# Moving elementwise sums to VectorE and reordering the start of the up projection

## The chip, the cores and the metric

The kernel runs on one core of one Trainium2 chip. The metric is the device time of one execution in microseconds (us), as the median of several runs; lower is better. Five engines work in a core, each through its own queue in order: TensorE (PE) multiplies matrices and writes PSUM, VectorE (DVE) and ScalarE (ACT) work element by element, GpSimd (POOL) does so too but reads no PSUM here, and SyncE (SP) issues the DMA transfers.

## The reference

One layer of a diffusion backbone with D = 1024, 1024 latent tokens and 256 context tokens. What comes ahead of the change (adaLN, input projection, mLSTM, windowed attention) is left as it is. What matters here is the end of the layer:

```python
x = x + g_a * (jnp.concatenate([y_m, y_a], axis=-1) @ w_out[l])
x = x + g_f * conv_glu(modulate(rmsnorm(x, norm_ffn[l]), sh_f, sc_f),
                       w_up[l], ffn_conv_w[l], ffn_conv_b[l], w_down[l])
...
def conv_glu(h, w_up, conv_w, conv_b, w_down):
    a, val = jnp.split(h @ w_up, 2, axis=-1)
    a = jax.nn.gelu(dwconv(a, conv_w, conv_b))
    return (a * val) @ w_down
```

`w_up` is 1024 x 5632, `w_down` 2816 x 1024, and the result is normed once more (`final_norm`).

## The kernel before, in words

**Products.** Every f32 operand is split into a high part (an fp32r copy, made on ACT) and a low part (the operand less its high part, made by a subtraction on VectorE or GpSimd). A product is three matmuls: high by high, high by low, low by high.

**The up projection** is done by a two by two scheme with seven products in place of eight. The features (1024) are cut into two halves and the tokens (1024) into two halves; the columns of `w_up` are taken in 22 blocks, each of 128 value columns and 128 gate columns. On the token side the seven operands lie in `hB` (high and low), in slots named B11, B21, B22, T1, T2, T3, T4. B11 and B21 belong to the first four token blocks, B22 to the last four; the T's are sums: `sum1` gives T1 = B12 - B11, `sum2` T2 = B22 - T1, `sum3` T3 = B22 - B12, `sum4` T4 = B21 - T2. `sum1` and `sum4` overwrite the raw tile of block b - 4, `sum3` that of block b. On the weight side a block arrives as `R`, two tiles (`Ra` with two parts, `Rb` with two parts and room for three more). `sums_v` makes two sums in `Rb`, `sums_g` two more; the second of `sums_g` overwrites the part `R[1][:, 1]`, which the first of `sums_v` reads. `wsplit` makes the high and low parts (`wh`, `wl`) of a pair of them: number 0 from `Ra`, 1 from the sums of `sums_v`, 2 and 3 from the rest.

**The loop over token blocks** (from L1450 on; order 1, 5, 2, 6, 3, 7, 4, with block 0 made ahead) does for block b half of the output projection (`wout_n`, 12 matmuls for each half n) and adds it to the residual x (L1361, VectorE); for the block before it the norm (`sq`, `norm_b`: squares and root on ACT, reciprocal on VectorE) and eight transposes (L1391); for the block before that the evacuation (`evac`, L1403 on ACT and L1405 on VectorE, into the raw tile) and the splits into `hB`. With a block of the second half (5, 6, 7) come its token sums. In the loop 5 and 6 have their turn; `split34`, the high and low parts of T3 and T4, runs an iteration later (`late`). Blocks 7 and 4 come behind the loop. The raw tiles of blocks 5 to 7 share one buffer, so the evacuation of block 7 waits until the low part of T3 of block 6 has been read.

**Behind the loop** come the first product of all (`ps_a`, B11), the last norm (block 4, one half on ACT, the other on VectorE, L1377), the transposes of block 4, `ps_a2`, the sums of the first weight block, and the first products f, c, b, e, d of block 0 (B22, T1, T2, T3, T4 in this order).

**Blocks 1 to 21.** Block i runs the products a, b, A, c, e, d, C on PE; A adds into a's PSUM and C into c's. VectorE makes `u2` from b, then in `av2` adds e (to `u3`) and c (to `av`). C writes into c's bank and so has to wait for `av2`. VectorE also does the sums and splits for block i + 1 and the conv, gate and products of block i - 1, with GpSimd taking `mul2` and the sums of `combine`.

**What sets the order.** From the token loop to the end PE, VectorE, ACT and GpSimd run in the order in which the code issues their instructions (a manual schedule called `fence`); SP does so from the first products on. A wait at the head of a queue holds all that is behind it.

Of the kernel before, what the change touches and what calls it, by code (L numbers as in the profile page):

```python
# [18 lines left out]
P = 128  # L19
# [59 lines left out]
def build(tc, I, out, dbg=None):  # L79
    nc = tc.nc  # L80
    dbg = dbg or {}
    V, S, G, T = nc.vector, nc.scalar, nc.gpsimd, nc.tensor
# [889 lines left out]
    for h in range(H):  # L972
# [3 lines left out]
        else:  # L976
            wq = [wkq]
            late = lambda: wq.append(load_split(I["w_q"][1], 256, lambda: pq.tile([P, 4, 256], F32, name="wr", tag="rga")))
# [75 lines left out]
    class Wout:  # L1054
# [21 lines left out]
        def lo(self):  # L1076
            r = lambda a: a[:].rearrange("p (j q) -> p j q", j=4)
            V.tensor_tensor(out=r(self.l), in0=self.src, in1=r(self.h).bitcast(F32), op=ALU.subtract)
# [161 lines left out]
    for t in range(n + 2):  # L1240
        blk, sub = divmod(t, 4)
# [75 lines left out]
    hB = [hbp.tile([P, 7, 4, 512], F32R, name=f"hB{i}") for i in range(2)]  # L1317
    tbk = ExitStack()
    tbp = tbk.enter_context(tc.tile_pool(name="tbp", bufs=1, side="right", reuse_waits="tile"))
    B11, B21, B22, T1, T2, T3, T4 = range(7)  # L1320
# [19 lines left out]
    sub = lambda e, o, x, y: e.tensor_tensor(out=o, in0=x, in1=y, op=ALU.subtract)  # L1340
# [3 lines left out]
    def ysplit_h(b, eng=G):  # L1344
        ys[b] = [t4.tile([P, 4, P], F32R, name=f"y{n}", tag=f"y{n}", bufs=3 if n == "h" else 2) for n in "hl"]
        eng.copy(ys[b][0][:], yslice(b)) if eng is S else eng.tensor_copy(ys[b][0][:], yslice(b))
# [8 lines left out]
    def wout_n(b, n):  # L1355
        ns = slice(512 * n, 512 * n + 512)
        po = pO.tile([P, 512], F32, name="po", tag="o")
        yh, yl = ys[b]
        for kt in range(4):
            mm3(po[:], yh[:, kt], yl[:, kt], wos[4 + kt][0][:, ns], wos[4 + kt][1][:, ns], kt == 0, kt == 3)  # L1360
        return lambda: V.tensor_tensor(out=xs[b][:, ns], in0=po[:], in1=xs[b][:, ns], op=ALU.add)  # L1361
# [31 lines left out]
    def evac(b, kts=None):  # L1393
        w = KT // len(pts[b])
        if b not in raws:
            raws[b] = (tbp.tile([P, 2, 4, P], F32, name="raw00") if b == 0 else
                       er[:].rearrange("p a (k t) -> p a k t", k=4) if b == 4 else
                       tbp.tile([P, 2, 4, P], F32, name="raw", tag=f"raw{b // 4}", bufs=RB1 if b > 4 else 2))
        for kt in kts or range(KT):
            ga, sh = ada2[:, 16 + kt:17 + kt], ada2[:, 8 + kt:9 + kt]  # L1400
            o, i_ = raws[b][:, kt // 4, kt % 4], pts[b][kt // w][:, kt % w]
            if kt // w % 2 == 0:
                S.activation(o, i_, AF.Identity, bias=sh, scale=ga)  # L1403
            else:
                V.tensor_scalar(out=o, in0=i_, scalar1=ga, scalar2=sh, op0=ALU.mult, op1=ALU.add)  # L1405
# [9 lines left out]
    def sum1(b):  # L1415
        sub(V, raws[b - 4][:, 0], raws[b][:, 0], raws[b - 4][:, 0])
# [5 lines left out]
    def sum3(b, e=V):  # L1422
        sub(e, raws[b][:, 0], raws[b][:, 1], raws[b][:, 0])

    def sum4(b, e=V):
        sub(e, raws[b - 4][:, 1], raws[b - 4][:, 1], tbs[b][:, 0])

    def sum34(b):
        sum3(b, G)
        sum4(b, G)  # L1430

    split_t1 = lambda b: split(V, b, T1, 1, raws[b - 4][:, 0:1])
    split_t2 = lambda b: split(V, b, T2, 1, tbs[b][:])
# [9 lines left out]
                sub(V, hB[1][:, blk:blk + 1, :, ts], src, hB[0][:, blk:blk + 1, :, ts].bitcast(F32))  # L1443
        return lo

    def prod(ps, wt, j, blk, first, last, kts=range(4)):
        for kt in kts:
            ks = slice(kt * P, kt * P + P)
            for (sw, part) in ((0, 0), (0, 1), (1, 0)):
                T.matmul(ps[:], wt[sw][:, j, ks], hB[part][:, blk, kt, :], start=first and kt == 0 and sw + part == 0,  # L1450
                         stop=last and kt == 3 and sw == 1, skip_group_check=not first)

    load_x(1)
    order = [1, 5, 2, 6, 3, 7, 4]
# [10 lines left out]
    late = None  # L1465
    last = order[-1]
    for i, b in enumerate(order):
        prev = order[i - 1] if i else None
        pp = order[i - 2] if i > 1 else 0 if i == 1 else None
        add0 = wout_n(b, 0)  # L1470
        if prev is not None:
            sq(prev, 1)
        if pp is not None:
            evac(pp)
        if prev is not None:
            norm_b(prev)
        if i + 2 < len(order):
            ysplit_h(order[i + 2])
        if i + 1 < len(order):
            ysplit_l(order[i + 1])  # L1480
        lo = split(V if b == last else G, pp, B11, 2, raws[pp][:], True) if pp is not None and pp < 4 else None
        add0()
        sq(b, 0)
        if lo:
            lo()
        if late and b != last:
            late()()
            late = None
        if pp is not None and pp >= 4:
            sum1(pp)  # L1490
            sum2(pp)
            sum34(pp)
            split(V, pp, B22, 1, raws[pp][:, 1:2])
            split_t1(pp)
            late = lambda a=pp: split34(a)
        add1 = wout_n(b, 1)
        trans(prev if i else 0)
        add1()
        if pp is not None and pp >= 4:
            split_t2(pp)  # L1500
        if b != last:
            nc.sync.dma_start(x2_d[b][:], xs[b])
        if i + 2 < len(order):
            load_x(order[i + 2])
    ps_a = pA.tile([P, 512], F32, name="pa", tag="a")
    prod(ps_a, e0, 0, B11, True, True)
    lo = late()
    sq(4, 1)
    norm_b(4, True)
    lo()  # L1510
    nc.scalar.dma_start(x2_d[4][:], xs[4])
    evac(7)
    trans(4, (4, 5, 6, 7))
# [12 lines left out]
    f = ExitStack()  # L1526
# [12 lines left out]
    def sums_v(R, e=V):  # L1539
        add(e, R[1][:, 2], R[1][:, 1], R[1][:, 0])  # L1540
        sub(e, R[1][:, 3], R[1][:, 2], R[0][:, 0])


    def sums_g(R, e=V):
        sub(e, R[1][:, 4], R[0][:, 1], R[1][:, 3])
        sub(e, R[1][:, 1], R[0][:, 0], R[1][:, 1])

    def wsplit(R, n, eng=V):
        src = (R[0][:], R[1][:, 2:4], R[1][:, 0:2], R[1][:, 4:5])[n]
        w = src.shape[1]  # L1550
        wt = [fw.tile([P, w, 512], F32R, name=f"w{n}{w}", tag=f"w{n}{w}", bufs=5 if w == 2 else 2) for n in "hl"]
        S.copy(wt[0][:], src)  # L1552
        sub(eng, wt[1][:], src, wt[0][:].bitcast(F32))
        return wt


    R = load_R(0)
    sums_v(R, G)
    sums_g(R, G)
    evac(4, range(4, 8))  # L1560
    sum1(7)
    split(V, 7, B22, 1, raws[7][:, 1:2])
    split(V, 4, B22, 1, raws[4][:, 1:2])
    wB = wsplit(R, 3)
    evac(4, range(4))
    sum1(4)
    wS = wsplit(R, 1)
# [9 lines left out]
    newp = lambda n: (pA if n == "a" else pB if n in "fb" else pC).tile([P, 512], F32, name="p" + n,  # L1577
                                                                    tag={"a": "a", "f": "b", "b": "b"}.get(n, "c"))
    ps0 = {n: newp(n) for n in "fcbed"}
    prod(ps0["f"], wB, 0, B22, True, True)  # L1580
    prod(ps0["c"], wS, 0, T1, True, True)
    prod(ps0["b"], wS, 1, T2, True, True)
    wA = wsplit(R, 2)
# [13 lines left out]
    R = load_R(blocks[1])  # L1597
# [105 lines left out]
    R = load_R(blocks[2])  # L1703


    for i in range(1, NF):
        last = i == NF - 1
        if i > 1:
            C = Block(i, W, B)
            C.pe("a")  # L1710
            C.sn_()
        W = {}

        def split_w(*ns):
            for n in ns:
                if not last:
                    W[n] = wsplit(R, n)

        if i == 1:
            C.pe("b")  # L1720
            C.u2_()
            split_w(0)
            Rn = load_R(blocks[3], (0,))
            B.vt_()
            B.taps()
            B.gelu()
            for n in "Aced":
                C.pe(n)
            C.av2()
            sums_v(R)  # L1730
            C.av1()
            split_w(1)
            B.mul1()
            B.mul2()
            C.ident_()
            sums_g(R)
            B.combine()
            split_w(2, 3)
            R = load_R(blocks[3], (1,), Rn)
            C.pe("C")  # L1740
            B = C
            continue
        B.vt_()
        B.taps()
        B.gelu()
        B.mul1()
        B.mul2()
        C.pe("b")
        C.u2_()
        if not last:  # L1750
            sums_v(R)
        split_w(0)
        C.pe("A")
        C.pe("c")
        if i == NF - 2:
            nc.sync.dma_start(er[:], I["w_down"][0:2 * P, 0:512].rearrange("(k p) f -> p k f", p=P))
            nc.sync.dma_start(ar0[:], act_d["a11", 0][:])
        B.combine()
        if last:
            split2(e0[0][:], e0[1][:], er[:])  # L1760
            split2(a0[0][:], a0[1][:], ar0[:])
        C.pe("e")
        C.pe("d")
        C.av2()
        if last:
            C.pe("C")
            break
        sums_g(R)
        split_w(1)
        Rn = load_R(blocks[i + 2], (0,)) if i < NF - 2 else None  # L1770
        split_w(2)
        C.av1()
        C.ident_()
        split_w(3)
        R = Rn and load_R(blocks[i + 2], (1,), Rn)
        C.pe("C")
        B = C
# [186 lines left out]
    for t, (p, ps, fresh) in enumerate(products):  # L1964
        for j in range(NP):
# [35 lines left out]
            if NP + 3 <= n < NP + 3 + NL:  # L2001
                b = n - NP - 3
# [9 lines left out]
        if p == "m4":  # L2012

            part = lambda f_, *bs: [lambda b=b: f_(b) for b in bs]
# [106 lines left out]
```

## Time and profile before

| | us |
|---|---|
| median of 3 runs | 1279.54 |
| lowest and highest run | 1278.59 and 1282.48 |
| profiled execution, from first to last instruction | 1281.0 |
| PE busy in it | 1240.8 (97%) |
| VectorE busy in it | 974.5 (76%) |
| GpSimd busy in it | 208.8 (16%) |

The profiled execution has no other time than its span. Its times run from its first instruction: the token loop lies at about 582 to 629 us, the first products of block 0 end near 658, block 2 lies at 677 to 701 and block 3 behind it. A row of the timeline has the start, the duration, the engine, the line, the operation, output and inputs by name, shapes, the count of merged instructions, and in brackets how long the engine had stood idle and what ended that. A group's duration of two merged instructions is that of both. The granted clock is a share of TensorE's full speed.

### The profile page before, as it was taken

What the parts mean: (1) busy time and instruction counts of PE and PEld (TensorE: products, weight loads), DVE (VectorE), ACT (ScalarE), POOL (GpSimd) and SP (SyncE); (2) the same over time, 40 slices, a digit from 0 to 9 for tenths busy, and PEclk for the clock granted to TensorE, in tenths of its full rate; (3) what the DMA queues carried; (4) which work ended last, traced back from release to release, by engine and by line L of the source; (5) the groups of instructions that cost most, each with busy time, mean ns of one, the idle gap of its engine ahead of it and who ended that gap; (6) DMA issues with size and microseconds to landing.
All of it is one profiled execution on the core that took longest, in us unless ns stands there. A gap on an engine that the chain in (4) does not pass through costs nothing.

```text
span 1281.0 us, 19212 instructions
## 1 busy us (share of the span) xinstructions
PE 1240.8 (97%) x7023; PEld 1060.6 (83%) x7023; DVE 974.5 (76%) x1679; ACT 638.1 (50%) x1308; POOL 208.8 (16%) x175
## 2 busy tenths in 40 slices
PE   6999999999999999999899999999999999999997
PEld 4799898999898888887677888888888888788886
DVE  5863687877887878776898777777777776867887
ACT  6632556464865777776644333333333334444435
POOL 1200000000001433232402311332321332001000
PEclk9999999999999999999999999999999999999999
DMA  9431544452254332103413222233222337975563
GB/s 361 180 122 35 141 137 143 123 168 77 84 183 162 134 116 67 67 34 132 135 63 110 105 99 95 104 119 108 101 100 99 106 108 261 345 264 172 194 199 135
DMA packets 90416, 175.63 MB, mean 137 GB/s; under 512 B 12938, under 2 KB 29522, under 8 KB 90322
## 3 DMA queue, kind: packets, MB, share of 16 engines
q1 hardware_dynamic: 90034, 173.63, 40.2%
q8 instruction: 55, 0.90, 0.3%
q10 hardware_dynamic: 288, 0.79, 0.2%
q14 instruction: 39, 0.32, 0.1%
HBM read 136.05 MB, written 38.33 MB: 136 GB/s over the span
## 4 chain that ended last, share of the span: by engine, by line
PE 78%; DVE 8%; ACT 5%; DMA 5%; issue 3%; POOL 1%; SPq 0%; DVEq 0%; ACTq 0%; POOLq 0%
PE pd L1958 14%; PE pa L1450 9%; PE pc L1450 9%; PE pp L588 6%; PE pe L1450 4%; PE pb L1450 4%; PE pd L1450 4%; PE u L1174 3%; PE pt L1151 2%; PE po L307 2%; PE pv L307 2%; PE pv L309 2%; PE pv L308 2%; PE po L309 2%; PE po L308 2%
## 5 line engine op out<-in xcount | busy, mean ns | idle before, releaser
L1552 ACT CAST wh<-Rb 128x1024 fp32r<-128x1024 f32 (+1 forms) x66 | 59.5, 903 | 147.7 <-PE pd L1450 83.0
L1958 PE MATMUL pd<-dh,al 128*128 128x512 f32 x296 | 115.4, 390 | 0.7 <-DVE al L1324 0.6
L1958 PE MATMUL pd<-dl,ah 128*128 128x512 f32 x296 | 115.2, 389 | 0.0
L1958 PE MATMUL pd<-dh,ah 128*128 128x512 f32 x296 | 115.2, 389 | 0.0
L1450 PE MATMUL pc<-hB,wh 128*128 128x512 f32 x344 | 107.1, 393 | 2.5 <-DVE av L1529 2.5
L1450 PE MATMUL pa<-hB,wh 128*128 128x512 f32 x336 | 103.6, 390 | 0.0
L1340 DVE TENSOR_TENSOR wl<-Rb,wh 128x1024 fp32r<-128x1024 f32 (+1 forms) x66 | 68.9, 1045 | 39.4 <-ACT wh L1552 38.8
L1660 POOL TENSOR_TENSOR tt<-vt,tt 128x512 f32<-128x512 f32 x22 | 29.5, 1341 | 325.6 <-ACT tt L1654 325.6
L588 PE MATMUL pp<-hl,wh 128*128 128x512 f32 x256 | 79.3, 405 | 0.0
L1450 PEld LDWEIGHTS pc<-hB,wh 128*128 128x128 f32 x344 | 65.3, 190 | 16.6 <-DVE av L1529 2.9
L307 PE MATMUL pv<-wh,hl 128*128 128x256 f32 x256 | 76.1, 297 | 0.5 <-ACT ym L601 0.5
L1450 PEld LDWEIGHTS pa<-hB,wh 128*128 128x128 f32 x336 | 63.2, 188 | 13.6 <-ACT sn L1624 0.4
L309 PE MATMUL pv<-wh,hl 128*128 128x256 f32 x256 | 72.3, 283 | 0.0
L308 PE MATMUL pv<-wl,hl 128*128 128x256 f32 x256 | 72.3, 282 | 0.0
L1450 PE MATMUL pc<-hB,wl 128*128 128x512 f32 x172 | 67.6, 393 | 0.0
L1958 PEld LDWEIGHTS pd<-dh,al 128*128 128x128 f32 x296 | 55.5, 188 | 12.8 <-DVE al L1324 1.4
L1958 PEld LDWEIGHTS pd<-dl,ah 128*128 128x128 f32 x296 | 55.6, 188 | 11.9 <-DVE dl L1324 0.3
L1450 PE MATMUL pa<-hB,wl 128*128 128x512 f32 x168 | 65.4, 389 | 0.0
L1958 PEld LDWEIGHTS pd<-dh,ah 128*128 128x128 f32 x296 | 55.6, 188 | 11.5
L1158 ACT CAST ph<-pt 128x512 fp32r<-128x512 f32 (+1 forms) x88 | 46.2, 525 | 27.0 <-PE pt L1151 26.8
L1139 POOL TENSOR_SCALAR p__4966<-p__4966,ss 128x512 f32<-128x512 f32 x1 | 0.7, 688 | 346.6 <-DVE ss L1136 346.6
L1450 PE MATMUL pe<-hB,wh 128*128 128x512 f32 x176 | 54.6, 390 | 0.4 <-DVE hB L1340 0.2
(1072 smaller groups left out, 3760.2 us busy)
## 6 DMA issues: line engine op xcount, KB each, us to landing
w<-in_w_ada_dram SPq DMA_DIRECT2D x64, 256.0 KB, 2.7
br<-in_w_down_dram SPq DMA_DIRECT2D x25, 512.0 KB, 6.6
Ra<-in_w_up_dram SPq DMA_DIRECT2D x22, 512.0 KB, 3.6
Rb<-in_w_up_dram SPq DMA_DIRECT2D x22, 512.0 KB, 3.5
ar<-act_s SPq DMA_DIRECT2D x44, 256.0 KB, 3.6
act_a<-tt SPq DMA_DIRECT2D x33, 256.0 KB, 2.0
act_s<-tt SPq DMA_DIRECT2D x33, 256.0 KB, 2.0
wr<-in_w_h_dram SPq DMA_DIRECT2D x16, 512.0 KB, 4.4
```

What stands on the lines that cost most here:

```text
L307: T.matmul(ps, st_hi, mv_hi, start=first, stop=False)
L308: T.matmul(ps, st_hi, mv_lo, start=False, stop=False)
L309: T.matmul(ps, st_lo, mv_hi, start=False, stop=last)
L588: T.matmul(pp[:, 512 * n:512 * n + 512], wkq[sw][:, kt, cs], hl[n][part][:, kt, :], start=kt == 0 and sw + part == 0, stop=kt == KT - 1 an ...
L1151: T.transpose(self.pt[i][:, (2 * kk + j) * P:(2 * kk + j + 1) * P], self.p[j][:, kb * P:(kb + 1) * P], ident[:])
L1158: S.copy(self.ph[i][:, :w], self.pt[i][:, :w])
L1174: T.matmul(self.u[:], vv[:, c, self.g], part[i][:, kk * 2 * P:(kk + 1) * 2 * P], start=kb + m == 0, stop=kb == last and m == 1)
L1340: sub = lambda e, o, x, y: e.tensor_tensor(out=o, in0=x, in1=y, op=ALU.subtract)
L1450: T.matmul(ps[:], wt[sw][:, j, ks], hB[part][:, blk, kt, :], start=first and kt == 0 and sw + part == 0, stop=last and kt == 3 and sw == 1 ...
L1552: S.copy(wt[0][:], src)
L1660: G.tensor_tensor(out=self.tt[:, h2_], in0=self.vt[:], in1=self.tt[:, h2_], op=ALU.mult)
L1958: T.matmul(ps[:], ac[sa][:, js], w[sw], start=first and n == 0, stop=last and n == 2, skip_group_check=not fresh)
```

## The change

It has five parts.

1. The third and fourth token sums of blocks 5 and 6 (`sum34`) go from GpSimd to VectorE, and from ahead of the B22 split to behind the low part of T2, which is behind the second add to x.
2. The late parts of T3 and T4 of block 6 are written as a whole, high and low, ahead of the last norm; the low ones stood behind the norm's half on VectorE.
3. Of the four sums of the first weight block three go from GpSimd to VectorE, behind the evacuation of block 7; GpSimd keeps the one that overwrites `R[1][:, 1]`. `sum1` of block 7 goes behind the weight part of the first product.
4. The first product of block 0 (f, B22) runs its twelve matmuls by parts: four high by high, then four with the low tokens, then four with the low weights; before, each of the four 128-feature slices ran its three in a row.
5. In block 2 alone, `sums_v` and the first weight split for block 3 go behind `av2`.

The core of the diff:

```diff
     def sum34(b):
-        sum3(b, G)
-        sum4(b, G)
+        sum3(b)
+        sum4(b)
...
-    def prod(ps, wt, j, blk, first, last, kts=range(4)):
-        for kt in kts:
-            ks = slice(kt * P, kt * P + P)
-            for (sw, part) in ((0, 0), (0, 1), (1, 0)):
-                T.matmul(ps[:], wt[sw][:, j, ks], hB[part][:, blk, kt, :], start=first and kt == 0 and sw + part == 0,
-                         stop=last and kt == 3 and sw == 1, skip_group_check=not first)
+    def prod(ps, wt, j, blk, first, last, by_part=False):
+        parts = ((0, 0), (0, 1), (1, 0))
+        for kt, (sw, part) in ([(kt, p_) for p_ in parts for kt in range(4)] if by_part else
+                               [(kt, p_) for kt in range(4) for p_ in parts]):
+            T.matmul(ps[:], wt[sw][:, j, kt * P:kt * P + P], hB[part][:, blk, kt, :],
+                     start=first and kt == 0 and sw + part == 0, stop=last and kt == 3 and sw == 1,
+                     skip_group_check=not first)
...
             sum1(pp)
             sum2(pp)
-            sum34(pp)
             split(V, pp, B22, 1, raws[pp][:, 1:2])
             split_t1(pp)
             late = lambda a=pp: split34(a)
...
         add1()
         if pp is not None and pp >= 4:
             split_t2(pp)
+            sum34(pp)
...
     prod(ps_a, e0, 0, B11, True, True)
-    lo = late()
+    late()()
     sq(4, 1)
     norm_b(4, True)
-    lo()
...
     R = load_R(0)
-    sums_v(R, G)
-    sums_g(R, G)
+    sums_v(R)
     evac(4, range(4, 8))
-    sum1(7)
+    sub(V, R[1][:, 4], R[0][:, 1], R[1][:, 3])
+    sub(G, R[1][:, 1], R[0][:, 0], R[1][:, 1])
     split(V, 7, B22, 1, raws[7][:, 1:2])
     split(V, 4, B22, 1, raws[4][:, 1:2])
     wB = wsplit(R, 3)
+    sum1(7)
...
-    prod(ps0["f"], wB, 0, B22, True, True)
+    prod(ps0["f"], wB, 0, B22, True, True, True)
...
         B.mul2()
         C.pe("b")
         C.u2_()
-        if not last:
-            sums_v(R)
-        split_w(0)
+        if i > 2:
+            if not last:
+                sums_v(R)
+            split_w(0)
...
         C.av2()
+        if i == 2:
+            sums_v(R)
+            split_w(0)
```

VectorE's order in the loop, in the iteration that sums block 5; the first row is the second add to x, the second T2's low part, and the last two the next norm's scale and the next evacuation:

```order
 L1361 TENSOR_TENSOR x_7611<-po,x_7611 128x512
 L1340 TENSOR_TENSOR hB_7461<-tb,hB_7460 128x4x128
+L1340 TENSOR_TENSOR raw<-raw 128x512
+L1340 TENSOR_TENSOR raw<-raw,tb 128x512
 L1370 TENSOR_SCALAR r_7710<-r_7710 128x1
 L1405 TENSOR_SCALAR raw<-pt,ada_65 128x128 x4
```

The two sums are new in VectorE's queue; the add to x keeps its place ahead of them.

VectorE's order from the last add to x to block 4's evacuation (`er` is block 4's raw tile; the two `hB` rows are the late low parts; L1377 is the norm's half; the `Rb` rows are weight sums):

```order
 L1361 TENSOR_TENSOR x_7816<-po,x_7816 128x512
+L1340 TENSOR_TENSOR hB_7461<-raw,hB_7460 128x4x128 x2
 L1370 TENSOR_SCALAR r_7916<-r_7916 128x1
 L1374 RECIPROCAL r_7916<-r_7916 128x1
 L1377 TENSOR_SCALAR hn<-x_7816,r_7916 128x512
-L1340 TENSOR_TENSOR hB_7461<-raw,hB_7460 128x4x128 x2
 L1405 TENSOR_SCALAR raw<-pt,ada_65 128x128 x4
+L1529 TENSOR_TENSOR Rb<-Rb 128x512
+L1340 TENSOR_TENSOR Rb<-Rb,Ra 128x512
 L1405 TENSOR_SCALAR er<-pt,ada_65 128x128 x2
-L1340 TENSOR_TENSOR raw<-raw 128x512
+L1340 TENSOR_TENSOR Rb<-Ra,Rb 128x512
```

The low parts went ahead of the norm, and three weight sums came in behind block 7's evacuation.

VectorE's order in block 2 (`u_8365` is `u2`, `u_8366` is `u3`; the `Rb` rows are the sums for block 3 and `wl` its first low part):

```order
 L1529 TENSOR_TENSOR u_8365<-pb,sn 128x512
-L1529 TENSOR_TENSOR Rb<-Rb 128x512
-L1340 TENSOR_TENSOR Rb<-Rb,Ra 128x512
-L1340 TENSOR_TENSOR wl_8372<-Ra,wh_8371 128x1024
 L1529 TENSOR_TENSOR u_8366<-pe,u_8365 128x512
 L1529 TENSOR_TENSOR av<-pc,u_8366 128x512
+L1529 TENSOR_TENSOR Rb<-Rb 128x512
+L1340 TENSOR_TENSOR Rb<-Rb,Ra 128x512
+L1340 TENSOR_TENSOR wl_8433<-Ra,wh_8432 128x1024
 L1340 TENSOR_TENSOR Rb<-Ra,Rb 128x512 x2
```

The two adds that C waits for now come first, and the three steps for block 3 behind them.

## The prediction

> **What bounds the kernel now.** I read the page first, then who TensorE (PE) waited for between 600 and 720 us, where all the edits lie, then the granted clock there.
>
> ```profile
> span 1281.0 us, 19212 instructions
> ...
> PE 1240.8 (97%) x7023; PEld 1060.6 (83%) x7023; DVE 974.5 (76%) x1679; ACT 638.1 (50%) x1308; POOL 208.8 (16%) x175
> ```
>
> PE is busy 97% of the span, so only time in which PE stands still, or runs slowly, can be won. The waits of PE (in total, times, longest):
>
> ```profile
> PE pc L1450 <- DVE av L1529: 2.5, 1, 2.5
> PE pt L1391 <- ACT hn L1379: 1.5, 3, 0.5
> PE pt L1391 <- DVE raw L1405: 1.3, 1, 1.3
> PE pf L1450 <- ACT wh L1552: 1.1, 1, 1.1
> PE po L307 <- DVE x L1361: 0.6, 1, 0.6
> PE pt L1391 <- DVE hn L1377: 0.6, 1, 0.6
> ```
>
> These six add to 7.6 us. Two of them cost more than their length. Busy time by stretch (length, PE, PEld, DVE, ACT, POOL, granted clock, DMA share, GB/s):
>
> ```profile
> 642.82:646.24 3.42, 3.42 (x10) 2.65 (x9) 3.35 (x5) 1.41 (x3) 0.00 (x0) 0.50 0.00 0
> 694.03:697.44 3.41, 1.08 (x5) 0.91 (x6) 3.38 (x6) 0.00 (x0) 0.00 (x0) 1.00 0.21 77
> 697.44:700.86 3.42, 3.42 (x10) 2.65 (x9) 3.02 (x4) 1.34 (x2) 0.00 (x0) 0.50 0.48 153
> 702.00:760.00 58.00, 58.00 (x257) 48.01 (x256) 43.51 (x48) 19.56 (x22) 12.52 (x8) 1.00 0.27 96
> ```
>
> After the 2.5 us wait (694 to 696) the clock is 0.50 for 3.42 us, and so it is after the waits of 1.3 and 1.1 us (643 to 646). From 702 on PE never stops. In the chain that ended last the slow stretch is a product of 12 matmuls that took 4.59 us where the same product of the next block took 2.72:
>
> ```profile
> 696.36 4.59 PE pc L1450 x12
> ...
> 717.33 2.72 PE pc L1450 x12
> ```
>
> ```profile
> 693.48 0.39 PE L1450 MATMUL pd<-hB,wl 128*128 128x512 f32 x1
> 696.36 0.73 PE L1450 MATMUL pc<-hB,wh 128*128 128x512 f32 x2 [2.49 <-DVE av L1529]
> ```
>
> So the stall in block 2 is worth 2.49 + (4.59 - 2.72) = 4.36 us. The half clock at 643 is different: there the product behind it waits for VectorE anyway.
>
> ```profile
> 652.68 0.50 PE L1450 MATMUL pe<-hB,wh 128*128 128x512 f32 x1 [0.23 <-DVE hB L1340]
> ```
>
> PE, slow clock included, was at pe before VectorE had written the low part of T3. Between the loop over token blocks and 652 us the end is set by VectorE's queue; each us that leaves this queue moves everything behind it.
>
> **Block 2.** VectorE, PE and GpSimd (POOL) there:
>
> ```profile
> 688.38 0.68 DVE L1529 TENSOR_TENSOR u<-pb,sn 128x512 f32<-128x512 f32 x1
> 689.32 1.72 DVE L1529 TENSOR_TENSOR Rb<-Rb 128x512 f32<-128x512 f32 x1 [0.26 <-DMA Rb<-in_w_up_dram]
> 691.07 1.67 DVE L1340 TENSOR_TENSOR Rb<-Rb,Ra 128x512 f32<-128x512 f32 x1
> 692.66 2.32 DVE L1340 TENSOR_TENSOR wl<-Ra,wh 128x1024 fp32r<-128x1024 f32 x1
> 694.90 0.68 DVE L1529 TENSOR_TENSOR u<-pe,u 128x512 f32<-128x512 f32 x1
> 695.61 0.69 DVE L1529 TENSOR_TENSOR av<-pc,u 128x512 f32<-128x512 f32 x1
> ```
>
> ```profile
> 690.99 0.62 PE L1450 MATMUL pd<-hB,wh 128*128 128x512 f32 x2
> ```
>
> ```profile
> 690.56 3.33 POOL L1340 TENSOR_TENSOR tt<-tt 128x512 f32<-128x512 f32 x2
> ```
>
> The two adds at 694.90 and 695.61 read products e and c; the seventh product writes into c and so waits for the second add. They stand behind two weight sums and a low part (5.6 us) that the next block wants. With the change they go first: e is complete as d starts (691.0, and its last matmul drains until some 691.2), two adds of 0.7 end at 692.6, and PE's d ends at 693.7: no wait. The 4.36 us go. What is late next: the sums start at 692.6 in place of 689.3. One is still beside POOL (1.72), one free (0.64), the low part free (1.21, below); they end near 696.1. The next steps started at 696.2 before, so VectorE is 0 to 0.6 us earlier, while PE is 4.36 earlier. Block 3 had slack for that:
>
> ```profile
> 708.56 1.03 DVE L1529 TENSOR_TENSOR Rb<-Rb 128x512 f32<-128x512 f32 x1
> ...
> 711.21 1.21 DVE L1340 TENSOR_TENSOR wl<-Ra,wh 128x1024 fp32r<-128x1024 f32 x1
> 714.64 0.69 DVE L1529 TENSOR_TENSOR u<-pe,u 128x512 f32<-128x512 f32 x1 [2.22 <-PE pe L1450]
> ```
>
> VectorE stood ready from 712.4 and waited 2.22 us for PE; then the adds took 1.4 us. With PE 4.36 earlier, the seventh product of block 3 comes at 717.33 - 4.36 = 713.0, and VectorE, ready at 711.8 to 712.4, ends the adds at 713.2 to 713.8: a new wait of 0.2 to 0.8 us; I take 0.6. Net gain 3.8 us; at most 4.36, and 2.7 if block 3's low part falls beside POOL (2.32 for 1.21, 1.1 more).
>
> The row behind the clock term is the 0.50 after 2.49 us of idle PE. The Trainium skill, TensorE: Matmul & The Clock Gate, section "Why this matters for your kernels", asks for PE gaps over some 3 us before the clock falls; by that rule the stall would be worth its 2.49 us alone, and the sum 1.9 us less. This trace differs from it twice, and the measurement decides.
>
> **The loop over token blocks.** The third and fourth token sums went to POOL in two iterations, and VectorE's low parts ran beside them:
>
> ```profile
> 605.99 1.79 POOL L1340 TENSOR_TENSOR raw<-raw 128x512 f32<-128x512 f32 x1 [4.39 <-DVE raw L1340]
> ```
>
> ```profile
> 606.61 3.42 DVE L1340 TENSOR_TENSOR hB<-raw,hB 128x512 fp32r<-128x512 f32 x2
> ...
> 622.72 2.72 DVE L1340 TENSOR_TENSOR hB<-raw,hB 128x512 fp32r<-128x512 f32 x2 [0.67 <-ACT hB L1410]
> ...
> 652.54 1.28 DVE L1340 TENSOR_TENSOR raw<-raw,tb 128x512 f32<-128x512 f32 x2
> ```
>
> A pair of 128x512 ops takes 1.28 us alone and 3.42 or 2.72 beside POOL. The change saves 3.42 - 1.28 + 2.72 - 1.28 = 3.6 us of VectorE and adds four sums, 2.6 us: net 1.0. Its y casts stay on POOL and may now fall beside the pairs; I take 0.7, bounds 0 and 1.0. PE's wait for x (0.6) goes, since the add comes ahead of the sums; the sums stand ahead of the next norm, so its waits for hn shrink less.
>
> **Low parts ahead of the last norm.** On VectorE, ScalarE (ACT) and POOL:
>
> ```profile
> 630.89 0.68 DVE L1361 TENSOR_TENSOR x<-po,x 128x512 f32<-128x512 f32 x1
> ...
> 632.89 1.55 DVE L1377 TENSOR_SCALAR hn<-x,r 128x512 f32<-128x512 f32 x1
> 634.35 3.47 DVE L1340 TENSOR_TENSOR hB<-raw,hB 128x512 fp32r<-128x512 f32 x2
> 637.75 1.36 DVE L1405 TENSOR_SCALAR raw<-pt,ada 128x128 f32<-128x128 f32 x4
> ```
>
> ```profile
> 632.36 0.29 ACT L1371 ACTIVATE r<-r 128x1 f32<-128x1 f32 x1
> ```
>
> ```profile
> 632.86 1.28 POOL L1529 TENSOR_TENSOR Rb<-Rb 128x512 f32<-128x512 f32 x1 [7.97 <-DMA Rb<-in_w_up_dram]
> ...
> 635.65 3.30 POOL L1340 TENSOR_TENSOR Rb<-Ra,Rb 128x512 f32<-128x512 f32 x2
> ```
>
> From the last add of x to the evacuation of block 7 are 637.75 - 630.89 = 6.9 us, with norm and low parts beside POOL's weight sums. Changed: add 0.6, low parts 1.3, the square root and its hand-overs 0.7, the norm's half 0.7 (as a free 128x512 op; 1.55 is its locked price) = 3.3. It saves 3.6, bounds 2.7 (norm still locked) and 3.9. The low parts delay the norm by 1.3; what they release, the buffer of block 7's evacuation, is then free ahead of it.
>
> **Weight sums.** Three of four come onto VectorE behind that evacuation; the one left on POOL rewrites a part that the first reads, so it can start only then, beside the second. Price 0.64 + 1.72 + 0.64 = 3.0; bounds 1.9 (no lock) and 4.1 (two). The data had landed at 632.86 and is now asked for near 634, so the load hides; behind its store on SP it even starts earlier. The row here is 1.72 for 0.64. The Trainium skill, SBUF — State Buffer, section "Who interferes with whom", has the second of two such operations wait for the whole of the first; POOL's 1.65 in front of 0.64 would make 2.3, and the sum 0.6 less. The trace has VectorE end sooner, so 1.72 stands.
>
> **At nothing:** the first product by parts. Twelve matmuls stay twelve; its four high ones can start before the low parts, but the next product waits for T1's low parts on VectorE, which hide it. If they did not, it would be worth the 1.1 us of pf's wait at most. Block 7's first sum goes behind the first low weight part: same count, same queue. A half-clock window may come back here (1.9 us); in the row at 652.68 PE had that loss and still waited, so it lies under VectorE.
>
> **Sum.** Transition 0.7 + 3.6 - 3.0 = 1.3, bounds -1.4 and 3.0. Block 2: 3.8, bounds 2.7 and 4.4. Together 5.1 us: the profiled execution's 1281.0 would become 1275.9. That execution lies 1.5 above the median, 1279.54; from the median the forecast is 1274.4, its own bounds 1272.2 and 1278.2.
>
> **Rivals.** A, the stall moves: block 3's low part is locked, the wait there is 1.7 us, and the clock halves after it (1.87). For it: the adds come right behind that part, and other blocks' waits are near. Against: waits of 0.6 were followed by no half clock. The gain is 4.36 - 3.57 + 1.3 = 2.1: 1277.4. Chance 0.11.
> B, the transition gives nothing: POOL's last weight sum and the y casts lock VectorE as often as before; 3.8 remain: 1275.7. Chance 0.11.
> C, the gap does not cause the half clock: then a half-clock window stays somewhere under PE, and 5.1 - 1.9 = 3.2: 1276.3. Against: both windows follow PE's longest waits. Chance 0.06. It is the clock page's rule, named above.
> D, slower: the long pairs are the operation's own time, not POOL's doing. Then the loop saves nothing and gains 2.6; the norm stretch saves 0.6 + 3.4 + 0.7 + 1.55 = 6.3 against 6.9, so 0.6; the weight sums cost 3 x 1.72 = 5.2. Sum +7.2 - 3.8 = +3.4: 1282.9, more if the clock halves again. It decides where the moved operations keep 1.7 each with POOL idle. Against: the sums at 652.54 took 0.64 each. Chance 0.06.
>
> **Numbers.** The forecast keeps 0.66. About 0.3% (3.8 us) is what a measurement of this kernel can tell from no change; faster means under 1275.7. Of the forecast some 0.58 lies there, of B half, of C a third: 0.66. Slower by as much has the worse half of D, 0.04; the rest, 0.30, is within. The range runs from 1272.2 to 1278.0: it takes in A, B, C and nearly all of the forecast's own bounds.
>
> **What would show it.** Right: no wait of PE for av in block 2, clock 1.00 there; pairs of low parts at 1.3 us in both iterations; from the last add of x to block 7's evacuation 3.3 us; pe 1.3 us earlier against the loop's start; a wait under 1 us at most in block 3. Wrong: a wait of PE for av over 1.5 us in block 3 (A), evacuation earlier but T3's low part not (B), a half-clock window with no wait before it (C), 1.7 us per moved sum with POOL idle (D).

## The result and the profile after

| | before | after |
|---|---|---|
| median, us (runs) | 1280.04 (10) | 1276.87 (10) |
| lowest and highest, us | 1278.59 and 1282.85 | 1275.65 and 1277.54 |
| ratio, 95% interval | | 0.9973 [0.9964, 0.9982] |
| span of the profiled execution, us | 1281.0 | 1275.1 |

By the ratio the change is worth 3.5 us, between 2.3 and 4.6. The two profiled spans differ by 5.9 us, and that is more than the change gives: the profiled execution of before was a slow one of its kind, for a reason that the experiments bring out.

Who PE waited for between 600 and 720 us, in the profile after (total, times, longest):

```profile
PE pt L1391 <- ACT hn L1379: 1.6, 2, 1.2
PE pc L1450 <- DVE hB L1340: 1.2, 1, 1.2
PE pf L1450 <- ACT wh L1552: 1.1, 1, 1.1
PE pc L1450 <- ACT hB L1410: 0.8, 1, 0.8
PE pe L1450 <- ACT hB L1410: 0.5, 1, 0.5
...
PE pa L1450 <- ACT sn L1625: 0.2, 1, 0.2
```

The wait for av is gone, in block 2 and in block 3 as well; block 3 has a wait of 0.2 us for ScalarE's copy `sn` in its place. Of the waits of block 0's first products, that of pf (1.1 us) was there before; those of pc (1.2 and 0.8) and the 0.5 of pe are new in the list. Before, PE ran part of them at a clock of 0.50 (642.8 to 646.2 us) and had no wait for pc. What they wait for is made by VectorE or copied by ScalarE from what VectorE made; the run evac_scalar below shows that VectorE's queue still sets the time here.

The rows of the timeline after that answer to those of before: the second add to x near 601 us, from which I count below, the two pairs of low parts in the loop, the last add to x and what follows it, product e of block 0, and block 2.

```profile
601.53 0.69 DVE L1361 TENSOR_TENSOR x<-po,x 128x512 f32<-128x512 f32 x1 [1.84 <-PE po L309]
607.14 1.29 DVE L1340 TENSOR_TENSOR hB<-raw,hB 128x512 fp32r<-128x512 f32 x2
607.73 1.17 POOL L1346 CAST yh<-yTa 128x512 fp32r<-128x512 f32 x1 [5.60 <-PE po L308]
622.33 1.29 DVE L1340 TENSOR_TENSOR hB<-raw,hB 128x512 fp32r<-128x512 f32 x2 [0.67 <-ACT hB L1410]
630.24 0.68 DVE L1361 TENSOR_TENSOR x<-po,x 128x512 f32<-128x512 f32 x1
630.84 1.28 DVE L1340 TENSOR_TENSOR hB<-raw,hB 128x512 fp32r<-128x512 f32 x2
632.81 0.49 DVE L1377 TENSOR_SCALAR hn<-x,r 128x512 f32<-128x512 f32 x1
633.21 1.36 DVE L1405 TENSOR_SCALAR raw<-pt,ada 128x128 f32<-128x128 f32 x4
635.39 1.66 POOL L1340 TENSOR_TENSOR Rb<-Ra,Rb 128x512 f32<-128x512 f32 x1 [19.47 <-DVE Rb L1529]
636.45 1.14 DVE L1340 TENSOR_TENSOR Rb<-Ra,Rb 128x512 f32<-128x512 f32 x1
650.54 0.50 PE L1450 MATMUL pe<-hB,wh 128*128 128x512 f32 x1 [0.23 <-DVE hB L1340]
689.01 0.69 DVE L1529 TENSOR_TENSOR u<-pe,u 128x512 f32<-128x512 f32 x1 [2.10 <-PE pe L1450]
689.74 0.69 DVE L1529 TENSOR_TENSOR av<-pc,u 128x512 f32<-128x512 f32 x1
```

Both pairs in the loop take 1.29 us, where one took 3.42 and the other 2.72. The low parts and the norm's half stand free (1.28, 0.49), and from the last add to block 7's evacuation are 633.21 - 630.24 = 2.97 us. Of the weight sums only the third meets GpSimd, 1.14 us. In block 2 VectorE waits 2.10 us for product e and then adds at once.

The clock after, by stretch (length, PE, PEld, DVE, ACT, POOL, granted clock, DMA share, GB/s), at the two places that were slow before:

```profile
642.40:645.80 3.40, 2.22 (x10) 1.63 (x10) 3.31 (x7) 1.57 (x4) 0.00 (x0) 1.00 0.00 0
693.00:696.50 3.50, 3.50 (x17) 2.90 (x16) 3.47 (x5) 1.50 (x2) 0.00 (x0) 1.00 0.19 43
```

### The profile page after: what moved, and what is told of

Same layout as the page of the kernel before. It is cut to its first block, busy times and chain, and to the rows that moved or that the text cites. A ratio compares the mean times of both kernels' runs of the same rounds, so it can differ in the third digit from the quotient of the medians.

```text
span 1275.1 us, 19212 instructions
## 1 busy us (share of the span) xinstructions
PE 1236.9 (97%) x7023; PEld 1058.1 (83%) x7023; DVE 969.3 (76%) x1686; ACT 637.9 (50%) x1308; POOL 197.1 (15%) x168
## 4 chain that ended last, share of the span: by engine, by line
PE 81%; DVE 7%; ACT 5%; DMA 4%; issue 2%; POOL 1%; SPq 0%; DVEq 0%; ACTq 0%; POOLq 0%
PE pd L1963 14%; PE pa L1450 9%; PE pc L1450 9%; PE pp L588 7%; PE pe L1450 5%; PE pd L1450 4%; PE pb L1450 4%; PE u L1174 3%; PE pt L1151 2%; PE pv L307 2%; PE pv L309 2%; PE pv L308 2%; PE po L307 2%; PE po L309 2%; PE po L308 2%
## 5 line engine op out<-in xcount | busy, mean ns | idle before, releaser
L1450 PEld LDWEIGHTS pc<-hB,wh 128*128 128x128 f32 x344 | 64.6, 188 | 16.1 <-DVE hB L1340 1.5
```

The lines of the kernel that those rows point to most:

```text
L1450: T.matmul(ps[:], wt[sw][:, j, kt * P:kt * P + P], hB[part][:, blk, kt, :], start=first and kt == 0 and sw + part == 0, stop=last and kt = ...
```

## The experiments

Two counts put the profiles side by side: how far product e of block 0 starts behind the add to x near 601 us (what the transition costs; e is counted from its matmul that waits for the low part of T3, the row shown for before and after), and how far the seventh product of block 3 starts behind that e (what block 2 costs). What lies ahead of the add moves by 3.5 us from one execution to the next (it came between 600.29 and 603.82 us), so spans are not compared. In the changed kernel the seventh product of block 3 starts at 711.23 us in the chain:

```profile
700.05 3.01 PE pa L1450 x12
...
711.23 2.72 PE pc L1450 x12
```

| profile | e behind the add | norm's half (L1377) | first sum in block 2 | wait for av | block 3's seventh behind e |
|---|---|---|---|---|---|
| before | 51.67 | 1.55 | 1.72 | 2.49 | 64.65 |
| b_again | 51.01 | 0.49 | 0.69 | 1.23 | 61.75 |
| block2_only | 51.62 | 1.47 | moved | none | 60.70 |
| rest_only | 49.03 | 0.49 | 0.69 | 1.28 | 61.81 |
| gap_fill | 51.04 | 0.49 | 0.69 | filled | 62.50 |
| lock_lost | 51.71 | 1.59 | 1.73 | 2.49 | 64.62 |
| lost_filled | 51.69 | 1.54 | 1.73 | 0.25 | 63.02 |
| loop_only | 49.68 | 0.72 | 1.75 | 2.48 | 64.63 |
| late_only | 49.92 | 0.95 | 0.68 | 1.14 | 61.63 |
| wsum_only | 50.81 | 0.49 | 0.69 | 1.14 | 61.63 |
| after | 49.01 | 0.49 | moved | none | 60.69 |
| no_by_part | 49.02 | 0.49 | moved | none | 60.72 |
| evac_scalar | 47.72 | 0.49 | moved | none | 60.75 |
| sums_vector | 49.78 | 0.49 | moved | none | 60.80 |

Beside the two kernels that fill the gap, the last column has three values: 60.7 (the sums moved), 61.7 (VectorE's first sum 0.69 us) and 64.6 (1.7 us).

**Where are 1.6 us of the forecast?** I had forecast 5.1 us and saw 3.5. The *phase* theory: the 2.5 us wait comes in every execution, the half clock behind it only in some. The rival, *given back*: block 2's gain is lost again further on.

**b_again** is the kernel before, unchanged.

> The kernel before, unchanged, once more. Theory (phase): the 2.5 us wait in block 2 comes in every execution, but the half-clock window behind it (1.9 us) only in some, as the window's place differs from run to run; then the spans of the runs spread over some 4 us, their median is 2 to 3 us under the 1281.0 of the profile shown, and this profile may show block 2 at full clock. Rival (given back): every execution pays the half clock; the profile shows 0.50 behind block 2 again and the spans lie together near 1281.

Measured: ratio 0.9996 [0.9988, 1.0005]. Its timeline, and the seventh products of blocks 2 and 3 in its chain (start, duration):

```profile
601.79 0.69 DVE L1361 TENSOR_TENSOR x<-po,x 128x512 f32<-128x512 f32 x1 [1.84 <-PE po L309]
652.80 0.50 PE L1450 MATMUL pe<-hB,wh 128*128 128x512 f32 x1 [0.23 <-DVE hB L1340]
689.20 0.69 DVE L1529 TENSOR_TENSOR Rb<-Rb 128x512 f32<-128x512 f32 x1
689.34 1.70 POOL L1529 TENSOR_TENSOR tt<-tt 128x512 f32<-128x512 f32 x1
689.93 1.66 DVE L1340 TENSOR_TENSOR Rb<-Rb,Ra 128x512 f32<-128x512 f32 x1
695.21 0.73 PE L1450 MATMUL pc<-hB,wh 128*128 128x512 f32 x2 [1.23 <-DVE av L1529]
```

```profile
695.21 3.02 PE pc L1450 x12
...
714.55 2.72 PE pc L1450 x12
```

Neither theory had this: the same program shows a wait of 1.23 us and no half clock. What differs stands in the rows at 689. GpSimd's add in the first profile:

```profile
689.20 1.28 POOL L1529 TENSOR_TENSOR tt<-tt 128x512 f32<-128x512 f32 x1
```

There VectorE waited 0.26 us for the transfer of `Rb`, this add began at 689.20, and VectorE's sum, 0.12 us behind it, took 1.72 us. Here the transfer was in, VectorE began 0.14 us ahead of GpSimd, its sum took 0.69, and GpSimd's add took 1.70 instead of 1.28. In these rows whoever starts first is not held up, and the other waits; this I call a lock. The Trainium skill, SBUF — State Buffer, section "Who interferes with whom", says so: for two such operations it is the order of issue that decides who blocks. These rows agree on who waits: in the first profile GpSimd's add ended at 689.20 + 1.28 = 690.48 and VectorE's sum 0.56 us later, a little less than the 0.69 us that it takes alone.

The norm's half (L1377) runs a second race of this kind with GpSimd's first weight sum. In the first profile GpSimd began 0.03 us ahead (632.86 against 632.89) and the half took 1.55 us; here the half began 0.11 us ahead (633.67 against 633.78) and took 0.49. In four of the six profiles in which the transition is that of before (before, block2_only, lock_lost, lost_filled) it was held up, and e comes at 51.6 to 51.7 us there against 51.0 in the other two. In lock_lost the two starts lie 0.02 us apart, VectorE's first, and VectorE was held up even so: at that distance the starts do not tell who waits.

**block2_only** and **rest_only** are part 5 alone on the kernel before, and the change without part 5.

```diff
 block2_only, on the kernel before; rest_only takes the same lines back from the changed one
-        if not last:
-            sums_v(R)
-        split_w(0)
+        if i > 2:
+            if not last:
+                sums_v(R)
+            split_w(0)
...
         C.av2()
+        if i == 2:
+            sums_v(R)
+            split_w(0)
```

> Part 5 alone on the kernel before. As forecast: PE's wait for av in block 2 gone, 3.8 us by the profile of before. Phase theory: 2.0 us (2.5 less a new wait of 0.6) in executions without the half clock, 3.8 in those with it; some 2.5 in the median (ratio 0.998). Given back: the profile shows 3.8 less at block 3 and less than 1 of it at the end.

Measured: ratio 0.9988 [0.9979, 0.9997], 1.5 us (0.4 to 2.7).

> Parts 1 to 4 without part 5. As forecast 1.3 us; by the two profiles 2.7 us to the start of product e of block 0. Phase theory: 1.3 to 2.7 us in the median (ratio 0.998 to 0.999), the block 2 wait of 2.5 us stays. Given back: no difference (1.000), and the wait in block 2 longer by what was won.

Measured: ratio 0.9982 [0.9974, 0.9991], 2.3 us (1.2 to 3.3). The two gains add up to the change's 3.5 within their intervals. Nothing is given back: in the profiles of before, of b_again and after, the stretch from block 3's seventh product to the end of the span lasts 563.7, 564.3 and 563.9 us.

**gap_fill** is the kernel before with ten matmuls that nobody reads, behind product d of block 2, so that PE does not idle.

```diff
         C.pe("d")
+        if i == 2:
+            dm = newp("b")
+            for x in range(10):
+                T.matmul(dm[:], C.W[2][0][:, 0, 0:P], hB[0][:, T4, 0, :], start=x == 0, stop=x == 9)
         C.av2()
```

> The kernel before with ten matmuls whose result nobody reads in the wait of block 2, so that PE does not stand idle there. Phase theory: the half-clock window behind block 2 is gone in all executions (clock 1.00), the end of the wait stays where it was: 0.5 to 1.5 us less than before in the median, 1.9 in executions that had the half clock. Rival (the gap does not cause the half clock): the window is still there or elsewhere, no difference.

Measured: ratio 1.0007 [0.9999, 1.0016]. The ten take 2.43 us, twice the usual wait, and the usual wait has no half clock behind it that they could save: the phase theory falls here too. The column has 62.50 for it against 61.75.

**Is the lost race the cause?** The *lock* theory: if GpSimd starts first at 689 us, the wait is 2.49 us and the clock halves; if VectorE does, it is 1.2.

**lock_lost** makes VectorE lose by a small operation ahead of the sums.

```diff
         C.u2_()
+        if i == 2:
+            V.tensor_tensor(out=C.u2[:, 0:128], in0=C.b[:, 0:128], in1=C.sn[:, 0:128], op=ALU.add)
         if not last:
             sums_v(R)
```

> The kernel before, with one VectorE operation of 128x128 added in block 2 that repeats a quarter of u2 (same operands, same result) ahead of the two weight sums. It costs VectorE some 0.2 us, and lets GpSimd's add start ahead of VectorE's first weight sum instead of with it. Lock theory (the 2.49 us wait of the first profile was that execution's lost race): the first weight sum takes 1.7 us and the next 1.7, PE waits for av 2.3 to 2.8 us in block 2, one clock window at 0.50 follows in many executions, and the kernel is 1.2 to 3 us slower than before. Rival (the order of the two starts does not matter, the wait of 2.49 came from the late transfer itself): the sums keep 0.7 to 1.0 us, PE waits 1.3 to 1.6 us, and the kernel is 0.1 to 0.4 us slower.

Measured: ratio 1.0016 [1.0007, 1.0025], 2.0 us slower (0.9 to 3.2). Its timeline and chain:

```profile
691.55 0.29 DVE L1751 TENSOR_TENSOR u<-pb,sn 128x128 f32<-128x128 f32 x1
691.65 1.28 POOL L1529 TENSOR_TENSOR tt<-tt 128x512 f32<-128x512 f32 x1
691.76 1.73 DVE L1529 TENSOR_TENSOR Rb<-Rb 128x512 f32<-128x512 f32 x1
693.52 1.67 DVE L1340 TENSOR_TENSOR Rb<-Rb,Ra 128x512 f32<-128x512 f32 x1
695.11 2.32 DVE L1340 TENSOR_TENSOR wl<-Ra,wh 128x1024 fp32r<-128x1024 f32 x1
```

```profile
698.81 4.60 PE pc L1450 x12
...
719.75 2.72 PE pc L1450 x12
```

No transfer was waited for, and all of the first profile is back: 1.73, 1.67, 2.32, the wait of 2.49, and 4.60 us for the seventh product. The lock theory holds; the rival, which gave the wait to the late transfer itself, falls. Seven profiles have block 2's sums in their old place with nothing added ahead of them; VectorE lost in two (before, loop_only), in both behind a wait of 0.2 to 0.3 us for the transfer. Only two of the seven are of the kernel before itself, so two in seven is a rough estimate of how often it loses. The time fits it: if a lost race costs 64.6 - 61.7 = 2.9 us, losing always instead of in two of seven costs 2.9 x 5/7 = 2.1 us, and lock_lost measured 2.0.

The next three kernels each do one of the first three parts alone. Do the parts add, or do they share one gain? Against the executions of before in which the norm's half took 0.49 us (51.0 us from the add to e), the whole change gains 2.0 us in the transition; against those in which it was held up, 2.7.

```diff
 loop_only
-        sum3(b, G)
-        sum4(b, G)
+        sum3(b)
+        sum4(b)
...
             sum1(pp)
             sum2(pp)
-            sum34(pp)
...
             split_t2(pp)
+            sum34(pp)
```

> The kernel before with the first part of the change alone: the third and fourth token sums on VectorE, at the end of the iteration. Additive theory (each part is worth alone what it was worth in the change): low-part pairs of 1.3 us, product e of block 0 1.2 us earlier against the second-half add of x near 601 us (50 us behind it), ratio 0.9991. Rival (the gain of the loop is taken up by the wait for the later low parts): e at 51 us behind that add, ratio 1.000.

Measured: ratio 0.9992 [0.9983, 1.0001]; both pairs 1.29 us; e at 49.68, 1.3 us earlier. As the additive theory had it, in the profile; the ratio alone does not show it.

```diff
 late_only
-    lo = late()
+    late()()
     sq(4, 1)
     norm_b(4, True)
-    lo()
```

> The kernel before with the second part alone: late low parts ahead of the last norm, all four weight sums still on GpSimd. Additive theory: from the last add of x to block 7's evacuation 3.0 us instead of 6.9, and product e 3 to 3.9 us earlier (47 to 48 us behind the add near 601), ratio 0.997 to 0.9975. Rival (the weight sums on GpSimd lock whatever VectorE does there, and the low weight parts wait for them): the low parts are free at 1.3 us but the evacuation and the norm fall beside GpSimd, the low part of the first weights waits for the fourth sum, and product e gains 1 us or less, ratio 0.999 to 1.000.

Measured: ratio 0.9990 [0.9982, 0.9999]; e at 49.92, 1.1 us earlier, where the additive theory had 3 to 3.9. Its timeline:

```profile
632.46 0.68 DVE L1361 TENSOR_TENSOR x<-po,x 128x512 f32<-128x512 f32 x1
633.06 1.28 DVE L1340 TENSOR_TENSOR hB<-raw,hB 128x512 fp32r<-128x512 f32 x2
...
635.90 1.36 DVE L1405 TENSOR_SCALAR raw<-pt,ada 128x128 f32<-128x128 f32 x4
637.19 2.99 POOL L1340 TENSOR_TENSOR Rb<-Ra,Rb 128x512 f32<-128x512 f32 x2
637.82 1.22 DVE L1340 TENSOR_TENSOR raw<-raw 128x512 f32<-128x512 f32 x1
638.96 1.77 DVE L1340 TENSOR_TENSOR hB<-raw,hB 128x512 fp32r<-128x512 f32 x1
```

The evacuation does come 3.44 us behind the last add to x. But GpSimd's sums go on until 640.2, and now two other operations of VectorE run into them: 1.22 and 1.77 us for some 0.68 each. The lock isn't removed; it is moved to what comes next.

```diff
 wsum_only
-    sums_v(R, G)
-    sums_g(R, G)
+    sums_v(R)
     evac(4, range(4, 8))
-    sum1(7)
+    sub(V, R[1][:, 4], R[0][:, 1], R[1][:, 3])
+    sub(G, R[1][:, 1], R[0][:, 0], R[1][:, 1])
...
     wB = wsplit(R, 3)
+    sum1(7)
```

> The kernel before with the third part alone: three of the four weight sums on VectorE, behind block 7's evacuation. Additive theory: the three sums cost VectorE 2.4 us and nothing comes back, product e 2.4 us later (53.5 us behind the add near 601), ratio 1.0015 to 1.002. Rival (the low parts and the norm lose their locks when GpSimd is idle there, so the part gives back what it costs): the pair of low parts takes 1.3 instead of 3.5 us, product e within 0.5 us of before, ratio 0.9995 to 1.0005.

Measured: ratio 0.9995 [0.9986, 1.0003]; e at 50.81, 0.2 us earlier. VectorE in its timeline:

```profile
633.85 1.29 DVE L1340 TENSOR_TENSOR hB<-raw,hB 128x512 fp32r<-128x512 f32 x2
```

The rival was right: the pair of low parts takes 1.29 us with GpSimd idle, 3.47 before, and that pays for the three sums. Alone the three parts bring 1.3, 1.1 and 0.2 us, 2.6 together; joined they bring 2.0. Two of them, late_only and wsum_only, free the same pair of low parts (3.5 us before, 1.3 in each of them), and that can be gained only once. That this overlap is the whole difference is not shown: no run has just these two.

**The fourth part, the clock, and two further versions.**

**no_by_part** is the changed kernel with block 0's first product tile by tile again.

```diff
-    prod(ps0["f"], wB, 0, B22, True, True, True)
+    prod(ps0["f"], wB, 0, B22, True, True)
```

> The changed kernel without its fourth part: block 0's first product again goes tile by tile. Theory (the part is worth nothing, since the second product waits for T1's low parts on VectorE): product e of block 0 starts 48.9 to 49.2 us behind the add of x near 601 us, as in the changed kernel, and the ratio to the kernel before is 0.997, within 0.0005. Rival (the part hides the wait for the last weight's low part): product e 0.7 to 1.1 us later, ratio 0.998.

Measured: ratio 0.9975 [0.9966, 0.9984]; e at 49.02 us, against 49.01. The part is worth nothing here.

**lost_filled** is lock_lost with the ten matmuls of gap_fill.

> The kernel of the run lock_lost with ten unread matmuls of 128x512 (some 2.3 us, into a free buffer) behind product d of block 2, so that TensorE works on through its 2.5 us wait for av and the wait itself stays. Theory (the idle time lowers the clock): no window at 0.50 near 697 us, the seventh product takes 2.7 us instead of 4.6, and the kernel is 1.0 to 1.9 us faster than lock_lost, which was 1.0016 of the kernel before: ratio 1.0001 to 1.0008. Rival (the clock falls for another reason): the window stays, ratio 1.0016 or more.

Measured: ratio 1.0008 [1.0000, 1.0017]. Its timeline, then the granted clock by stretch:

```profile
688.61 1.73 DVE L1529 TENSOR_TENSOR Rb<-Rb 128x512 f32<-128x512 f32 x1
...
692.99 2.43 PE L1769 MATMUL pb<-hB,wh 128*128 128x512 f32 x10
695.66 0.73 PE L1450 MATMUL pc<-hB,wh 128*128 128x512 f32 x2 [0.25 <-DVE av L1529]
```

```profile
697.40:700.90 3.50, 3.50 (x17) 2.92 (x16) 2.37 (x3) 1.56 (x2) 0.00 (x0) 1.00 0.48 150
```

VectorE is as late as in lock_lost, but PE has not idled, and the clock stays at 1.00: block 3's seventh product comes 63.02 us behind e instead of 64.62. So 1.6 us of the lost race are the clock's, and the idle time causes it, as far as one filled profile against three unfilled ones can show; the intervals of the two ratios overlap, and the columns carry this. The Trainium skill, TensorE: Matmul & The Clock Gate, section "Why this matters for your kernels", warns of gaps over some 3 us; in block 2 2.48 to 2.49 us was enough in three profiles of three, and 1.14 to 1.28 us was not in four of four. The length of one gap is not the whole rule: near 640 us waits of 1.1 to 1.3 us and less, close together, have a clock of 0.50 behind them in before and b_again, and waits of 0.8 and 1.2 us in the changed kernel have not. What sets the limit no run here shows.

**evac_scalar** takes 0.97 us more from VectorE: ScalarE alone evacuates the half of block 4 that comes second (`range(4)`), and the third token sums stand ahead of the second weights' low part.

```diff
-            if kt // w % 2 == 0:
+            if kt // w % 2 == 0 or all_s:
...
-    evac(4, range(4))
+    evac(4, range(4), True)
...
-    wA = wsplit(R, 2)
     sum3(7)
     sum3(4)
+    wA = wsplit(R, 2)
```

> The changed kernel with 0.97 us less on VectorE between the norm and product e: ScalarE evacuates all of block 4's second half (VectorE's two operations of 0.72 us in total go), and the third token sums of blocks 7 and 4 stand ahead of the second weights' low part, where VectorE idles 0.25 us for ScalarE. Theory (VectorE's queue alone sets product e): e 0.6 to 1.0 us earlier, ratio 0.9966, a third of a us to one us faster than the changed kernel. Rival (ScalarE's casts are nearly as late as VectorE, and take over): e 0.2 us earlier or later, no difference to the changed kernel.

Measured: ratio 0.9966 [0.9954, 0.9979], median 1275.71 us in five runs; e at 47.72 us, 1.3 us earlier than after. VectorE's queue set e, as the theory said, and a little more came than I had counted. In time it is level with or ahead of the changed kernel: the intervals overlap, so it is shown that it beats the kernel before, and not that it beats the changed one.

**sums_vector** gives VectorE the fourth weight sum too.

```diff
-    sub(G, R[1][:, 1], R[0][:, 0], R[1][:, 1])
...
-    wA = wsplit(R, 2)
     sum3(7)
     sum3(4)
+    sub(V, R[1][:, 1], R[0][:, 0], R[1][:, 1])
+    wA = wsplit(R, 2)
```

> The changed kernel with the fourth weight sum on VectorE too, behind the third token sums, so that GpSimd does none of them. Theory (locks cost VectorE more than the sums do only while GpSimd works beside it): the third weight sum falls from 1.14 to 0.69 us, product c starts 0.45 us earlier, the sum adds 0.69 ahead of product e, less the 0.25 us of idle time that the new order fills: e within 0.1 us of the changed kernel, no difference in the time. Rival (VectorE's sum costs its whole 0.69 on e): 0.4 to 0.7 us slower than the changed kernel.

Measured: ratio 0.9985 [0.9975, 0.9995]; e at 49.78, 0.77 us later than after. Its timeline:

```profile
650.04 1.05 ACT L1552 CAST wh<-Rb 128x1024 fp32r<-128x1024 f32 x1 [2.56 <-DVE Rb L1340]
651.12 1.23 DVE L1340 TENSOR_TENSOR wl<-Rb,wh 128x1024 fp32r<-128x1024 f32 x1 [1.11 <-ACT wh L1552]
...
653.60 0.50 PE L1450 MATMUL pe<-hB,wh 128*128 128x512 f32 x1 [0.92 <-DVE hB L1340]
```

My expectation of no difference was wrong. The sum on VectorE comes late, ScalarE's cast waits 2.56 us for it, and VectorE then idles 1.11 us for the cast, which I had not counted. GpSimd's one sum, early and with one lock of 0.45 us, is the better place. The ratio lies 1.5 us above that of the changed kernel, of which these rows explain 0.8; the rest lies within the intervals.

## Why the prediction came out as it did

The time fell within the range and the sign was right. The forecast gain was 5.1 us and the measured one 3.5, because one term was too large; another was too small and hid part of it. That the time lies in the range all the same is in part luck: the two errors have opposite signs. The call that had 0.66, a median under 1275.7, did not come true; it was 1276.87, though the ratio's interval lies below 1.

**Block 2 (3.8 us): the mechanism right, the size that of one execution.** "So the stall in block 2 is worth 2.49 + (4.59 - 2.72) = 4.36 us" holds for the execution shown: it took 64.65 us from e to block 3's seventh product, the changed kernel 60.69, a gain of 3.96. But by the seven profiles most executions win the race and take 61.7, and there the same edit is worth 1.0, under the bound of 2.7 that I gave the term. With two lost in seven, an estimate of the mean is (2 x 3.96 + 5 x 1.0) / 7 = 1.8; block2_only measured 1.5 (0.4 to 2.7). The step that failed is the one that carried the whole stall over to the median: "from the median the forecast is 1274.4". There was a sign of it. I set the span of the profiled execution against the median of times and called it 1.5 above. In the other profiled executions the time was 1.7 to 2.3 us longer than the span, so by estimate this one took about 1283 us, some 3 us over the median. It had lost both races, that of block 2 (2.9 us) and that of the norm's half (51.67 - 51.01 = 0.66).

**The new wait in block 3 (0.6 us for av)** did not come. VectorE's adds ended at 709.96 + 0.69 = 710.65 us, ahead of the seventh product at 711.23. Instead PE waited 0.19 us for `sn`, with a product of 3.01 us behind it in place of 2.72: 0.5 us. The size was near by luck.

**The loop (0.7 us)** gave 1.17: the last add to x came 630.89 - 601.01 = 29.88 us behind the first, now 630.24 - 601.53 = 28.71. A y cast did fall beside the first pair (607.73 us), but it started second, and the pair kept its 1.29 us. My upper bound of 1.0 counted VectorE's operations alone; PE's wait for x, 0.6 us, which went too, may be the rest.

**The low parts ahead of the norm (3.6 us)** gave 6.86 - 2.97 = 3.89 against the execution shown, the upper bound, in part since the norm's half ran free (0.49 us; I had taken 0.7). Against b_again, where it took 0.49 already, it is 5.81 - 2.97 = 2.84.

**The weight sums (-3.0 us)** cost 2.40 from the evacuation to e (17.33 against 14.93 us), 2.00 against b_again. One lock cost 1.14 - 0.69 = 0.45 us and not 1.08: VectorE's sum came when GpSimd had only 637.05 - 636.45 = 0.60 us left (635.39 + 1.66 = 637.05).

**The transition (1.3 us)** so gave 2.66 against the execution shown and 2.00 against b_again: 0.7 to 1.4 us more than forecast, which made up for part of block 2's surplus.

**By parts, at nothing:** e did not move without the part (no_by_part). A half-clock window did not come back at 643 us.

**The rivals.** A (the stall moves to block 3): no wait for av there. B (the transition gives nothing): rest_only gained 2.3 us. C (the gap does not cause the half clock): lost_filled speaks against it. D (the long pairs are the operation's own time): 1.29 us with GpSimd away. The measured 3.5 us lies between the gains that B and C forecast, 3.8 and 3.2, but not for their reasons.

## What to carry to other kernels

Look at a stall in a second profile before you take it off the median: when two engines start within some 0.2 us of each other and one holds up the other, which of them wins can differ between executions. A profiled execution that lies well above the median may carry such a loss. And a lock is not removed by moving one of its two sides out of the way: see what the other engine runs into next.

## What the hardware showed that I had not expected

A late transfer of 0.26 us cost 2.9 us: it lost the race by 0.12 us, VectorE's first sum took 1.72 us instead of 0.69 (the two operations behind it took the same in both), PE's wait grew from 1.23 to 2.49 us, and that brought a stretch of half clock, 1.6 us more. The gap doubled and the cost quadrupled (1.0 against 3.96 us).

VectorE's scaling of 128x512 in SBUF (L1377) took 0.49 us free, or when it began 0.11 us ahead of GpSimd (b_again), and 0.72 to 1.59 where it was held up beside GpSimd, while its evacuations from PSUM took 1.36 us whether GpSimd was at work or not (637.75 us before, 633.21 after).
